# Two sums of weights from DRAM for one unit of a feed-forward layer, and other starting points for all such sums

## The chip, the cores and the metric

The kernel runs on one core of one Trainium2 chip. The metric is the device time of one execution in microseconds, as the median of several runs. The core has TensorE (PE in the profile; its weight loads are PEld), VectorE (DVE), ScalarE (ACT), GpSimd (POOL) and the queue of SyncE (SP), which issues most of the DMAs. The DMAs of all queues run on the core's 16 DMA engines.

## The reference

The reference computes two layers of an encoder over 256 positions of width 2048, in float32. Layer 0 mixes positions by pooling and attention, layer 1 by a bidirectional mLSTM; each is followed by the same kind of gated feed-forward block:

```
def conv_ffn(x, w_up, conv_w, conv_b, w_down):
    u = x @ w_up
    up = jnp.pad(u, ((0, 0), (1, 1), (0, 0)))
    c = conv_w.astype(u.dtype)
    u = c[0] * up[:, :-2] + c[1] * up[:, 1:-1] + c[2] * up[:, 2:] + conv_b.astype(u.dtype)
    gate, val = jnp.split(u, 2, axis=-1)
    return (jax.nn.silu(gate) * val) @ w_down
```

`w_up` is 2048 x 11264, `w_down` 5632 x 2048. The change concerns the product `x @ w_up` of both layers, and in layer 0 how one fifth of a part of it gets its weights.

## The kernel before

**Weights.** All weights are float32 and are streamed once, in 890 chunks of 128 x 1024 (512 KB), by the class `Stream`. `load` issues the DMA of a chunk from SP (L93 where the chunk is put together from parts, L99 else). `split` turns it into a high part (a rounding cast on ScalarE, L152) and a low part (a subtraction on VectorE, L153); both are multiplied, so that each product is three matmuls (high x high, high x low, low x high). Loads run 5 to 7 chunks ahead of TensorE, splits 2 to 3.

**Order.** TensorE's instructions stand in the order in which the code writes them. VectorE, ScalarE, SP and POOL are ordered by a scheduler that estimates times, except where the code says `keep_in_program_order`.

**Layers in terms of loads.** Loads 0 to 79 are the attention layer's, 80 to 403 the first feed-forward layer's, 404 to 565 the mLSTM layer's, 566 to 889 the second feed-forward layer's.

**Units.** Most of the up-projection goes column block by column block (`up`, tile `up`). Five groups of four column blocks per layer, the units, go in another way (`quads`, tile `p`): the product of 2 x 2 blocks is made with seven block products instead of eight, from sums of blocks of the activations (tile `sx`) and sums of blocks of the weights. For each of eight pairs of rows a unit has the four weight blocks b11, b12, b22, b21 side by side in the input `in_q` (128 x 2048), and needs

- an even chunk: b11 and s1 = b11 + b12,
- an odd chunk: s2 = b22 + s1 and s3 = b21 + s2,
- a left chunk: b12 + b22 beside b22 (one addition on VectorE, L140), and every two pairs a last chunk without sums.

**Where the sums are made.** `UNITS` lists the five units of each layer; the last number of an entry, in the code `made` or `kind`, says where. With 2, all three sums s1, s2, s3 are made in DRAM ahead of time: SP copies blocks of the input into a buffer G in DRAM (L121, L123), and POOL issues DMAs that add to it (L124 for s1 in two halves of 64 partitions, L128 for s2 and for s3). The even chunk is then loaded as b11 from the input and s1 from G, the odd chunk whole from G. With 3, as the third unit of layer 0 has it, only s1 is made in DRAM, and the odd chunk is loaded raw (b22, b21) and gets its sums by two additions on VectorE, one after the other (L142, L143):

```
if kind == "chain":
    pin(add(l, l, self.sum))
    pin(add(r, r, l))
```

**When the sums are made.** `places` gives for each pair a load and a gap; the pair's four steps (first half, second half, s2, s3) are issued right behind the loads number at, at + gap, at + 2 gap and at + 3 gap, by `make_step`. SP only copies; each accumulate on POOL waits for the copies, or for the accumulate before it, and everything behind it on POOL waits too. In the attention and mLSTM layers POOL also does the small power operations of the norms (L275). A load that reads G waits on SP for its accumulate.

## Time and profile before

| | |
|---|---|
| median of 3 runs | 2162.97 us (2162.5 to 2164.91) |
| the profiled execution | 2164.07 us, span 2162.3 us |
| TensorE busy | 2155.0 us |
| VectorE, ScalarE, POOL busy | 1716.1, 1308.5, 276.0 us |
| bytes by DMA | 596.15 MB |
| of those by POOL's queue | 59.00 MB |
| mean granted TensorE clock | 0.999 |

The page of the profile has the engines' busy times, the DMA queues and the costliest groups of instructions. A row of a group names line, engine, operation and tile, the shapes and the count, then busy time and mean duration, then the idle time of the engine before these instructions and what ended it. A row of the timeline begins with the start and the length in microseconds. A row of the windows gives a stretch, its length, for each engine busy time and count, and at the end the granted clock, the mean busy share of the 16 DMA engines and the GB/s that they moved. An arrow `<-` names what a thing was made from, or what an engine waited for.

### The profile page before, as it was taken

The numbers are of one execution on the slowest core, as the hardware profiler recorded it, in microseconds if no ns is written. First come the engines' busy times: TensorE is split into PE (matmuls) and PEld (weight loads), VectorE is DVE, ScalarE is ACT, GpSimd is POOL, SyncE is SP. The second block draws the span as 40 slices with busy tenths as digits, with TensorE's granted clock in tenths as the row PEclk, the third lists the DMA queues.
The fourth block names the chain that finished last, engine by engine and source line by source line (L and its number), as shares of the span: only waits on it lengthen the run. The fifth ranks groups of instructions, "written<-read, shape, count | busy, mean of one in ns | idle before, by whom it ended". The sixth has DMA issues, their size and how long they took to land.

```text
span 2162.3 us, 31058 instructions
## 1 busy us (share of the span) xinstructions
PE 2155.0 (100%) x10896; PEld 1827.3 (85%) x10896; DVE 1716.1 (79%) x2400; ACT 1308.5 (61%) x1840; POOL 276.0 (13%) x344
## 2 busy tenths in 40 slices
PE   9999999999999999999999999999999999999999
PEld 7888888888888888889888888888888888888887
DVE  7686698989888797866777676669898888879785
ACT  7665566766556576656554544456676666757663
POOL 0222111211111111101111111110000000000000
PEclk9999999999999999999999999999999999999999
DMA  9878899999999999979899988877999999877773
GB/s 327 256 226 247 253 262 329 336 329 315 311 328 297 360 312 348 315 207 249 250 268 247 259 249 247 259 243 223 312 284 309 301 294 291 272 253 235 260 244 119
DMA packets 204702, 596.15 MB, mean 276 GB/s; under 512 B 26010, under 2 KB 28354, under 8 KB 204546
## 3 DMA queue, kind: packets, MB, share of 16 engines
q1 hardware_dynamic: 167776, 531.43, 70.1%
q0 software_dynamic: 33696, 59.00, 18.6%
q10 hardware_dynamic: 3074, 3.75, 0.9%
q8 instruction: 85, 1.39, 0.2%
q14 instruction: 71, 0.58, 0.1%
HBM read 591.93 MB, written 119.58 MB: 329 GB/s over the span
## 4 chain that ended last, share of the span: by engine, by line
PE 99%; DVE 1%; issue 0%; ACT 0%; DVEq 0%; ACTq 0%
PE up L268 25%; PE dn L268 21%; PE p L268 17%; PE op L268 8%; PE mv L268 4%; PE mk L268 4%; PE mq L268 4%; PE mo L268 4%; PE qproj L268 3%; PE kproj L268 1%; PE pool L268 1%; PE vproj L268 1%; PE tr L1081 1%; PE av L268 1%; PE qk L268 1%; PE end L268 1%
## 5 line engine op out<-in xcount | busy, mean ns | idle before, releaser
L153 DVE TENSOR_TENSOR hl<-w,hl 128x1024 fp32r<-128x1024 f32 (+2 forms) x892 | 1074.0, 1217 | 323.0 <-ACT hl L152 309.0
L152 ACT CAST hl<-w 128x1024 fp32r<-128x1024 f32 (+2 forms) x891 | 923.5, 1048 | 641.3 <-PE dn L268 105.0
L268 PE MATMUL up<-xx,hl 128*128 128x512 f32 (+1 forms) x3072 | 560.7, 337 | 0.0
L268 PEld LDWEIGHTS up<-xx,hl 128*128 128x128 f32 x3072 | 486.8, 188 | 76.7
L268 PE MATMUL dn<-hl,g 128*128 128x512 f32 x2064 | 492.0, 391 | 0.0
L268 PEld LDWEIGHTS dn<-hl,g 128*128 128x128 f32 x2064 | 386.1, 188 | 79.4
L268 PE MATMUL p<-hl,sx 128*128 128x512 f32 x960 | 250.4, 390 | 1.9 <-DVE hl L153 1.9
L124 POOL DMA_DIRECT2D G<-in_q x160 | 132.1, 827 | 881.0 <-DMA G<-in_q 877.4
L268 PEld LDWEIGHTS p<-hl,sx 128*128 128x128 f32 x960 | 175.9, 188 | 36.6 <-DVE hl L153 2.9
L128 POOL DMA_DIRECT2D G<-G x144 | 127.3, 884 | 530.7 <-DMA G<-in_q 228.2
L268 PE MATMUL p<-hl,xx 128*128 128x512 f32 x720 | 193.7, 391 | 0.0
L268 PEld LDWEIGHTS p<-hl,xx 128*128 128x128 f32 x720 | 131.1, 188 | 24.2
L268 PE MATMUL mk<-xx,hl 128*128 128x512 f32 (+1 forms) x512 | 92.5, 338 | 0.0
L268 PE MATMUL mq<-xx,hl 128*128 128x512 f32 (+1 forms) x512 | 92.2, 337 | 0.0
L268 PE MATMUL mv<-hl,xx 128*128 128x512 f32 (+2 forms) x480 | 91.7, 350 | 0.0
L268 PE MATMUL op<-hl,cat 128*128 128x512 f32 x384 | 91.6, 393 | 0.0
L268 PE MATMUL mo<-hl,xx 128*128 128x512 f32 x384 | 90.5, 391 | 0.0
L268 PE MATMUL op<-hl,mcat 128*128 128x512 f32 x384 | 89.5, 392 | 0.0
L268 PEld LDWEIGHTS mq<-xx,hl 128*128 128x128 f32 x512 | 79.3, 188 | 11.6
L268 PEld LDWEIGHTS mk<-xx,hl 128*128 128x128 f32 x512 | 79.0, 188 | 11.7 <-DVE hl L153 0.4
L268 PEld LDWEIGHTS mv<-hl,xx 128*128 128x128 f32 x480 | 78.3, 189 | 11.2
L268 PEld LDWEIGHTS op<-hl,mcat 128*128 128x128 f32 x384 | 71.5, 188 | 14.6
(242 smaller groups left out, 1861.5 us busy)
## 6 DMA issues: line engine op xcount, KB each, us to landing
w<-in_up SPq DMA_DIRECT2D x192, 512.0 KB, 6.2
w<-in_dn SPq DMA_DIRECT2D x176, 512.0 KB, 6.1
w<-in_m_in SPq DMA_DIRECT2D x124, 512.0 KB, 5.9
w<-in_q SPq DMA_DIRECT2D x88, 512.0 KB, 6.3
G<-in_q SPq DMA_DIRECT2D x144, 256.0 KB, 6.5
G<-G POOLq DMA_DIRECT2D x144, 256.0 KB, 7.5
w<-G SPq DMA_DIRECT2D x72, 512.0 KB, 6.5
w<-in_a_in SPq DMA_DIRECT2D x46, 512.0 KB, 6.1
```

The source lines that it names most:

```text
L124: pin(add.dma_start(G[r, 0:512], src[r, 512:1024], accum_op=ALU.add))
L128: pin(add.dma_start(G[:, at : at + 512], G[:, of : of + 512], accum_op=ALU.add))
L152: (self.nc.vector.tensor_copy if i + c == 0 else self.nc.scalar.copy)(hl[:, 0, c : c + n], w[:, c : c + n])
L153: self.nc.vector.tensor_sub(hl[:, 1, c : c + n], w[:, c : c + n], hl[:, 0, c : c + n].bitcast(F32))
L268: pe.matmul(out_, lhsT, rhs, start=start, stop=stop, skip_group_check=True)
L1081: pe.transpose(tr[:, j, t * P : t * P + P], src[:, c : c + P], ident)
```

## The change

A fourth value of `made` is introduced and given to the third unit of layer 0. With 4, s1 and s2 are made in DRAM. The copy of the first two steps also takes b22 (a further 128 KB each), step three adds s1 to it, step four does nothing. The odd chunk is loaded in two parts of 256 KB, s2 from G and b21 from the input, and VectorE makes s3 with one addition. The even chunk stays as it was.

The places of all pairs of layer 0 and of the first 28 pairs of layer 1 are changed as well. In layer 0 the first pair begins behind load 16 in place of 24, and the steps of the first unit follow every 5.5 loads in place of 6.5, of the second every 8 in place of 9, of the third every 6 in place of 4 with a gap of 3 in place of 2, of the fourth every 10 as before and 8 loads sooner, of the fifth every 9 in place of 8. Of layer 1's pairs, 4 in place of 7 begin in the first feed-forward layer, and 24 in place of 21 in the mLSTM layer; the last 12 stay.

```diff
-        if kind in ("made", "have"):
+        if kind in ("made", "have", "half"):
...
                 pin(sync.dma_start(G[r, 0:512], src[r, 0:512]))
-                if kind == 2:
-                    pin(sync.dma_start(G[r, 1024:2048], src[r, 1024:2048]))
+                if kind in (2, 4):
+                    to = 2048 if kind == 2 else 1536
+                    pin(sync.dma_start(G[r, 1024:to], src[r, 1024:to]))
                 pin(add.dma_start(G[r, 0:512], src[r, 512:1024], accum_op=ALU.add))
-        elif kind < 3:
+        elif kind < 3 or kind == 4 and part == 2:
...
+            if kind == "half":
+                pin(add(r, r, l))
...
-    ((1, 1, 17, 38, 2), (2, 1, 45, 64, 2), (3, 1, 71, 97, 3), (4, 1, 104, 127, 2), (5, 1, 134, 157, 2)),
+    ((1, 1, 17, 38, 2), (2, 1, 45, 64, 2), (3, 1, 71, 97, 4), (4, 1, 104, 127, 2), (5, 1, 134, 157, 2)),
...
-                seq.append(("made", ((key, 2, 4),)) if made in (1, 2) else ("chain", q[:, 1024:2048]))
+                seq.append(("half", ((key, 2, 3), q[:, 1536:2048])) if made == 4 else
+                           ("made", ((key, 2, 4),)) if made in (1, 2) else ("chain", q[:, 1024:2048]))
...
-    places = [[(24 + 13 * k // 2, 3) for k in range(8)] + [(76 + 9 * k, 4) for k in range(8)]
-              + [(150 + 4 * k, 2) for k in range(8)] + [(180 + 10 * k, 5) for k in range(8)]
-              + [(264 + 8 * k, 4) for k in range(8)]]
+    places = [[(16 + 11 * k // 2, 3) for k in range(8)] + [(60 + 8 * k, 4) for k in range(8)]
+              + [(122 + 6 * k, 3) for k in range(8)] + [(172 + 10 * k, 5) for k in range(8)]
+              + [(256 + 9 * k, 4) for k in range(8)]]
     at = len(weights) + len(ml)
-    places.append([(at - 240 + 11 * k, 5) for k in range(7)] + [(at - 162 + 38 * k // 5, 4) for k in range(21)]
+    places.append([(at - 220 + 14 * k, 5) for k in range(4)] + [(at - 164 + 20 * k // 3, 4) for k in range(24)]
                   + [(at + 17 * k, 8) for k in range(12)])
```

## The prediction

> **What bounds the kernel now.** First the page, for the engines and the DMA queues.

> ```profile
> PE 2155.0 (100%) x10896; PEld 1827.3 (85%) x10896; DVE 1716.1 (79%) x2400; ACT 1308.5 (61%) x1840; POOL 276.0 (13%) x344
> q1 hardware_dynamic: 167776, 531.43, 70.1%
> q0 software_dynamic: 33696, 59.00, 18.6%
> ```

> TensorE is busy for 2155.0 of 2162.3 us. A change elsewhere pays only where TensorE waits or its clock falls, and costs only where it makes TensorE wait. Second, the waits of TensorE and of its weight loads (us in total, times, longest).

> ```profile
> PE p L268 <- DVE hl L153: 1.9, 1, 1.9
> PEld mk L268 <- DVE hl L153: 0.4, 1, 0.4
> ```

> Behind the start there is one true stall: a product of a four-column unit (tile p) waits 1.9 us for VectorE's low half of a split chunk. Third, the two feed-forward layers over like stretches, from a like piece of up-projection to a like piece: columns are length, busy us and instructions of PE, PEld, DVE, ACT, POOL, then clock, DMA share and GB/s.

> ```profile
> 357.36:906.84 549.48, 547.59 (x2702) 461.79 (x2701) 474.29 (x617) 351.20 (x452) 90.36 (x112) 1.00 1.02 327
> 1550.76:2096.22 545.46, 545.46 (x2701) 460.82 (x2701) 464.92 (x600) 350.87 (x450) 30.09 (x37) 1.00 0.87 277
> 568.00:572.00 4.00, 2.11 (x9) 1.43 (x8) 4.00 (x6) 0.97 (x4) 1.61 (x2) 0.94 1.05 353
> 572.00:576.00 4.00, 4.00 (x13) 3.11 (x13) 2.40 (x3) 1.86 (x2) 0.00 (x0) 0.63 1.01 253
> ```

> The same TensorE work (2702 and 2701 matmuls) takes 549.48 us in the first layer and 545.46 in the second: 4.02 us more. They lie in the last two rows: 1.89 us of idleness between 568 and 572, and behind it a lowered clock, 4 us at 0.94 and 4 at 0.63, which is 4 x 0.06 + 4 x 0.37 = 1.72 us of lost matmul time. That is 3.61; the rest of the 4.02 is smaller hiccups. The first layer's DMA engines are full (share 1.02), the second's are not (0.87). Fourth, VectorE's order before the stall.

> ```profile
> 562.76 0.68 DVE L142 TENSOR_TENSOR w<-w,w 128x512 f32<-128x512 f32 x1
> 564.16 1.22 DVE L153 TENSOR_TENSOR hl<-w,hl 128x1024 fp32r<-128x1024 f32 x1
> 565.29 0.68 DVE L143 TENSOR_TENSOR w<-w 128x512 f32<-128x512 f32 x1
> 566.69 2.35 DVE L153 TENSOR_TENSOR hl<-w,hl 128x1024 fp32r<-128x1024 f32 x2
> 568.96 0.68 DVE L142 TENSOR_TENSOR w<-w,w 128x512 f32<-128x512 f32 x1
> 569.56 1.22 DVE L153 TENSOR_TENSOR hl<-w,hl 128x1024 fp32r<-128x1024 f32 x1
> 570.83 0.30 PEld L268 LDWEIGHTS p<-hl,sx 128*128 128x128 f32 x2 [2.31 <-DVE hl L153]
> ```

> L142 and L143 are the two chained additions of an odd chunk of the third unit. They are 2.53 us apart, another chunk is split between them, and the split that TensorE waits for ends at 569.56 + 1.22 = 570.78.

> **The change, part by part.**

> (1) One addition less per odd chunk. The group rows for the chain are these.

> ```profile
> L142 DVE TENSOR_TENSOR w<-w,w 128x512 f32<-128x512 f32 x8 | 5.5, 683 | 0.0
> L143 DVE TENSOR_TENSOR w<-w 128x512 f32<-128x512 f32 x8 | 5.5, 684 | 0.1
> ```

> VectorE loses 8 x 0.683 = 5.5 us of work. On the late path lie two of the eight, at 562.76 and 568.96, worth 1.37 us: alone they leave 1.89 - 1.37 = 0.5 us of the stall. But the chunk is also whole after one addition, at about 563.4 rather than at 565.29 + 0.68 = 565.97, so its split can go 2.5 us sooner, in its own turn. 1.37 + 2.5 is over 1.89, so I take the stall as gone. The end on the other side: 0.5 us of idleness stays and lowers the clock again for 1.7, leaving a gain of 4.0 - 2.2 = 1.8. With both ends, 1.8 to 4.0; I take 4.0. What is late next is the following odd chunk:

> ```profile
> 572.87 2.36 DVE L153 TENSOR_TENSOR hl<-w,hl 128x1024 fp32r<-128x1024 f32 x2 [0.82 <-ACT hl L152]
> 580.45 0.53 PEld L268 LDWEIGHTS p<-hl,sx 128*128 128x128 f32 x3
> ```

> Its split ends at 572.87 + 1.2 = 574.1, with two additions in front of it; TensorE takes it at 580.45, or 4.0 sooner without the stall, at 576.4. That still fits.

> Does the clock belong to the stall? The row 572 to 576 says so: 0.63 directly behind 1.89 us of idleness, 1.00 elsewhere in the stretch. [...]

> (2) The odd chunk becomes two transfers, one half from the input, one from G. Rows of both sizes:

> ```profile
> w<-in_q SPq DMA_DIRECT2D x88, 512.0 KB, 6.3
> w<-in_q SPq DMA_DIRECT2D x80, 256.0 KB, 5.9
> w<-G SPq DMA_DIRECT2D x80, 256.0 KB, 6.3
> ```

> Two halves land no later than a whole (5.9 and 6.3 against 6.3). SP issues 8 more; the G half waits for its POOL sum, whose last step now stands 65 to 81 loads ahead of it. Cost nothing, hidden by the loads ahead; if that cover were gone, everything behind it on SP would wait.

> (3) A second sum in DRAM: per pair one copy (two halves of 128 KB more from SP) and one 256 KB accumulate on POOL. The price of DMA time follows from q1 and q0: 0.701 x 2162.3 / 531.43 = 2.85 us of all sixteen engines per MB copied, 0.186 x 2162.3 / 59.00 = 6.82 per MB accumulated. A pair adds 0.262 MB of each: 2.53 us, eight pairs 20.3 us. The issues fall into two queues, SP's (first row: what it waits for, total, times, longest) and POOL's (count | busy, mean ns | idle before):

> ```profile
> SPq L99 <- DVE hl L153: 1048.7, 569, 6.9
> L128 POOL DMA_DIRECT2D G<-G x144 | 127.3, 884 | 530.7 <-DMA G<-in_q 228.2
> ```

> SP waits 1048.7 us for free buffers, so 16 more small copies, and copies moved to other places, cover none of its useful time. POOL mostly stands waiting for its own copies; in the feed-forward layer only further sums are queued behind it, so eight more cost TensorE nothing by themselves.

> (4) Sums begun at other times. A full pair (three blocks of 0.262 MB copied and three accumulated) costs 7.6 us, a new pair of the third unit 5.1, an old one 2.5. Per load that is: second unit 0.84 before (one in 9 loads), 0.95 after (one in 8); third unit 0.63 before (one in 4), 0.85 after (one in 6). Loads 100 to 176 are used by TensorE from about 311 to 470 us (matmuls counted along its instructions). Loads 100 to 122 gain 22 x 0.11 = 2.4 us, 150 to 176 gain 26 x 0.22 = 5.7, and at the change-over last steps of the second unit fall beside first ones of the third, by my count 1 us: some 9 in all. Three pairs, 23 us, move from the end of the first feed-forward layer into the mLSTM layer. Where the load is heaviest:

> ```profile
> 324.00:378.00 54.00, 54.00 (x270) 45.70 (x269) 44.40 (x54) 34.41 (x43) 8.87 (x11) 1.00 1.04 330
> 690.00:770.00 80.00, 80.00 (x384) 67.22 (x384) 64.69 (x77) 47.64 (x57) 13.87 (x17) 1.00 1.05 347
> w<-in_up SPq DMA_DIRECT2D x16, 512.0 KB, 9.3
> w<-in_up SPq DMA_DIRECT2D x12, 512.0 KB, 10.1
> 351.18 1.22 DVE L153 TENSOR_TENSOR hl<-w,hl 128x1024 fp32r<-128x1024 f32 x1
> 354.25 1.77 PEld L268 LDWEIGHTS dn<-hl,g 128*128 128x128 f32 x8
> PEld p L268 <- DVE hl L153: 0.4, 1, 0.4
> ```

> Rows three and four are the landing times within 320 to 400 and within 690 to 770; then one chunk of the tight place, split by 352.40 and first used at 354.25, so 2 us ready; last, the only wait of a weight load in 340 to 400. The engines are full in 324 to 378 and TensorE is not idle. In 690 to 770 the fifth unit's sums are already begun every 8 loads, at a share of 1.05 and landings of 10.1 us, and TensorE is busy in all 80 us. So 9 us more, spread over 160, is most likely paid from the loads' lead. Bounds: 0 to 9 us of lateness, less the 2 us by which chunks lie ready there. I take 0, nearest to the 690 to 770 row, which has this density.

> (5) Attention. The first copies go out behind load 16, the second of the four in the first row below, at about 28 us, and not behind load 24; their accumulate on POOL then stands ahead of the small power operations there.

> ```profile
> 26.66 9.62 SPq L99 DMA_DIRECT2D w<-in_a_in  x4
> x<-in_xn SPq DMA_DIRECT2D x4, 512.0 KB, 9.5
> 28.00:46.00 18.00, 18.00 (x81) 14.93 (x80) 12.52 (x24) 15.14 (x39) 1.76 (x3) 1.00 0.93 357
> 45.90 2.45 POOL L275 TENSOR_TENSOR ry_qk<-rv_qk,mhalf 128x8 f32<-128x8 f32 x1
> 50.39 1.29 DVE L516 TENSOR_TENSOR rot_k<-rot_k,re_qk 128x512 f32<-128x512 f32 x2
> 52.47 0.60 PE L525 MATMUL tr_k<-cst,rot_k 128*128 128x128 f32 x4
> ```

> The keys' scale ends on VectorE at 51.68, TensorE takes it at 52.47: 0.8 us of room. A copy that lands in some 10 us, as the blocks of x do just before it, is there by 38, and its accumulate is out of POOL's way. The second half goes with load 19, near 38, and lands by 48 at the latest. If its accumulate is put ahead of ry_qk, that is up to 48 + 0.9 - 45.9 = 3 us late, and TensorE 2.2; if behind, nothing. I take 0: in the code the operation comes before load 19.

> (6) mLSTM. One spot has no room:

> ```profile
> 1015.12 1.15 DVE L829 SCALAR_TENSOR_TENSOR arg<-G,mc,kml 128x256 f32<-128x256 f32 x3 [1.21 <-DMA G<-gd]
> 1016.79 1.22 DVE L153 TENSOR_TENSOR hl<-w,hl 128x1024 fp32r<-128x1024 f32 x1
> ```

> VectorE waits for the gates' broadcast, and the split behind it is the one that a weight load awaits for 0.4 us. A later broadcast passes straight to TensorE; an earlier one gains at most those 0.4. The sums there are denser by one in seven: 0.4 gained to 2 lost; I take 0, as the copies also fall on other loads.

> Sum: -4.0. Against the profiled execution, 2164.07 - 4.0 = 2160.07. That execution lies 1.10 above the median of the runs; if the 4.0 come off the median whole, 2158.97. I take the middle, **2159.5 us**, 0.16% faster, inside the 0.2% (4.3 us) that a measurement can tell from no change. Even the whole 4.02 is 0.19%.

> **Rivals.**

> The loads become late (slower). Place: first and second unit of the first layer, loads 100 to 176. With the engines full, the 9 us pass on; 2 us are eaten by the chunks that lie ready; 7 reach TensorE in two stalls, each with a lowered clock of 1.7: 10.4 lost, 4.0 gained, 2162.97 + 6.4 = 2169.4; I take 2168.5, as some of it is made up where the share falls. For it: share 1.04 and the weight load that already waits 0.4 us. Against it: the 690 to 770 row. It decides once 4.9 us reach TensorE (4.9 + 3.4 - 4.0 = 4.3). Chance 0.24.

> The stall shrinks or moves: the third unit's one addition is again placed late in VectorE's order, or another chunk takes its place. 0.5 us idle plus the clock: 2162.97 - 1.8 = 2161.2, and no gain, 2163, if a full stall comes back. Chance 0.16.

> Only the idleness counts. If the lowered clock was particular to the profiled run, the gain is 1.9: 2161.1. For it: the runs shown spread from 2162.5 to 2164.91. [...] Against it: the clock row. Chance 0.10.

> A small new stall in attention or mLSTM (parts 5 and 6), 1 to 2 us with or without the clock: 2159.5 + 2 = 2161.5. Chance 0.10.

> **How the numbers follow.** My forecast has 0.40, by itself 2158.0 to 2161.0. Faster by over 0.2% means below 2158.6: only the low end of my own case, 0.11. Slower means above 2167.3: the late loads and a little of two others, 0.26. Within: 0.63. The range runs from 2158.2 (4.0 off the median and 0.8 of the runs' spread) to 2169.0, just past the late-load case; about 0.06 below and 0.13 above are left out.

> **What would show it.** Right: no wait of PE p on DVE hl around 570, clock 1.00 there, a stretch from 357 to 907 of about 545.5 us; one addition of 0.68 per odd chunk, VectorE 5.5 us less busy; accumulates G<-G 152 instead of 144, 2.1 MB more in each of q0 and q1; waits for loads in 320 to 400 longer, TensorE not idle. Wrong: a new PE wait between 340 and 480 with a lowered clock behind it; PE idle at tr_k near 52 or at mk near 1018; the p wait still there with the split of the odd chunk out of turn.

## The result, and the profile after

The changed kernel takes 2169.05 us (median of 17 runs, 2165.02 to 2173.56), the kernel before 2164.04 on the same chip (17 runs, 2162.5 to 2167.82). The ratio is 1.0023 with a 95% interval of 1.0016 to 1.0031: 5 us slower. Forecast were 2159.5, and 2169.0 as the range's upper end. The runs of the changed kernel also lie further apart, over 8.5 us against 5.3.

The page of the changed kernel first (engines with share of the span and instructions; the two main DMA queues with packets, MB and share).

```profile
PE 2155.3 (99%) x10896; PEld 1827.1 (84%) x10896; DVE 1710.9 (79%) x2392; ACT 1308.0 (60%) x1840; POOL 282.7 (13%) x352
q1 hardware_dynamic: 170208, 533.52, 70.3%
q0 software_dynamic: 34848, 61.10, 19.0%
```

What the change does to the work is as forecast: VectorE 5.2 us less, eight accumulates more on POOL, 2.1 MB more in each queue. TensorE is busy as long as before, in a span that is 4.4 us longer (2166.7). The waits of TensorE, by line and releaser (us in total, times, longest):

```profile
PE p L271 <- DVE hl L156: 2.5, 3, 1.1
PE up L271 <- DVE xx L337: 1.7, 2, 1.2
PE npr L271 <- DVE dg L363: 0.5, 1, 0.5
PE ov L271 <- DVE pt L572: 0.5, 1, 0.5
PE ov L271 <- ACT pt L571: 0.5, 1, 0.5
```

In place of one stall of 1.9 us there are these smaller ones, and a further row of 0.2 us (p <- ACT hl). Tile ov is a product of the attention, up one of the up-projection, p one of a unit; npr carries the layer norm's scale. Both kernels also wait 1.2 us at their start (wps). The like stretches of the two feed-forward layers (columns as in the prediction), and the place of the old stall, which now lies 4.4 us later:

```profile
361.72:911.32 549.60, 546.85 (x2701) 460.57 (x2701) 469.37 (x610) 351.32 (x452) 80.80 (x100) 1.00 1.00 321
1555.37:2100.87 545.50, 545.50 (x2702) 460.81 (x2701) 464.90 (x600) 350.90 (x450) 30.07 (x37) 1.00 0.86 277
572.00:576.00 4.00, 4.00 (x20) 3.30 (x19) 4.00 (x7) 2.64 (x4) 0.79 (x1) 1.00 1.07 351
576.00:580.00 4.00, 4.00 (x20) 3.30 (x18) 2.54 (x4) 1.98 (x3) 0.00 (x0) 1.00 0.99 314
```

The old stall is gone, and its lowered clock: TensorE is busy at 1.00 in all 8 us. Yet the first layer's stretch is no shorter, 549.60 against 549.48: 2.75 us of new idleness stand in it. And it begins 361.72 - 357.36 = 4.36 us later. So all of the profiled 4.4 us are lost ahead of this stretch, and within it the gain from the old stall is given back. Matched chunk by chunk (the first matmul of a load's chunk in both traces), TensorE comes 1.3 us later than in the kernel before to load 82, 4.4 later to loads 90 to 130, 8.3 later to loads 145 to 220, and 4.5 later from load 230 on. Where, the order of time shows: first TensorE ahead of the stretch, then POOL and VectorE, then the weight loads in the stretch.

```profile
158.79 0.39 PE L271 MATMUL ov<-pt,vt 128*128 128x256 f32 x1 [0.51 <-ACT pt L571]
159.70 0.50 PE L271 MATMUL ov<-pt,vt 128*128 128x256 f32 x2 [0.53 <-DVE pt L572]
...
268.29 0.96 PE L271 MATMUL up<-xx,hl 128*128 128x512 f32 x4 [1.24 <-DVE xx L337]
269.80 0.67 PE L271 MATMUL npr<-dg,cst 128*128 128x256 f32 x2 [0.54 <-DVE dg L363]
...
272.36 0.85 PE L271 MATMUL up<-xx,hl 128*128 128x512 f32 x3 [0.51 <-DVE xx L337]
```

```profile
264.90 0.79 POOL L125 DMA_DIRECT2D G<-in_q  x1 [8.87 <-DMA G<-in_q]
265.43 1.00 POOL L278 TENSOR_TENSOR ry_n<-rv_n,mhalf 128x2 f32<-128x2 f32 x1
266.47 0.16 DVE L280 TENSOR_TENSOR re_n<-ry_n 128x2 f32<-128x2 f32 x1 [5.45 <-POOL ry_n L278]
```

```profile
382.79 0.99 PEld L271 LDWEIGHTS p<-hl,sx 128*128 128x128 f32 x5 [1.39 <-DVE hl L156]
...
393.95 0.99 PEld L271 LDWEIGHTS p<-hl,sx 128*128 128x128 f32 x5 [1.26 <-DVE hl L156]
...
404.39 1.00 PEld L271 LDWEIGHTS p<-hl,sx 128*128 128x128 f32 x5 [0.90 <-DVE hl L156]
```

Three places, then: 158 (about 1 us more than before), the layer norm at 266 to 272 (about 3 us, 2.3 of them as plain idleness in these rows), and the second unit of the first feed-forward layer at 381 to 404 (about 4 us). At the layer norm POOL has stood 8.87 us on an accumulate that waits for its copy; behind it stands ry_n, the power operation of the layer norm's scale, whose input VectorE had written by 261.0, and which runs at 265.43. VectorE, which needs its result next, stands 5.45 us, and TensorE then waits for VectorE's xx. In the kernel before the operation runs in front of the accumulate that comes next:

```profile
260.05 0.72 POOL L275 TENSOR_TENSOR ry_n<-rv_n,mhalf 128x2 f32<-128x2 f32 x1 [3.83 <-DVE rv_n L273]
265.26 0.86 POOL L124 DMA_DIRECT2D G<-in_q  x1 [4.50 <-DMA G<-in_q]
```

Scale of the comparisons below: three kernels that were taken twice came back within 0.1, 0.4 and 1.3 us, and the 95% intervals against the kernel before reach some 2 us to either side. A difference of less than 2 us between two of the kernels is therefore not shown by itself, and pieces of the change do not add up more closely than that.

### The profile page after: what moved, and what is told of

It is laid out like the page before. It is cut to its first block, busy times and chain, and to the rows that moved or that the text cites. A ratio compares the mean times of both kernels' runs of the same rounds, so it can differ in the third digit from the quotient of the medians.

```text
span 2166.7 us, 31105 instructions
## 1 busy us (share of the span) xinstructions
PE 2155.3 (99%) x10896; PEld 1827.1 (84%) x10896; DVE 1710.9 (79%) x2392; ACT 1308.0 (60%) x1840; POOL 282.7 (13%) x352
## 4 chain that ended last, share of the span: by engine, by line
PE 91%; DMA 6%; DVE 2%; ACT 1%; issue 0%; POOL 0%; ACTq 0%; SPq 0%; DVEq 0%; POOLq 0%
PE up L271 23%; PE dn L271 21%; PE p L271 16%; PE op L271 7%; PE mo L271 4%; PE mk L271 4%; PE mq L271 4%; PE mv L271 4%; PE qproj L271 3%; DMA w<-in_up 1%; PE kproj L271 1%; DMA w<-in_q 1%; PE vproj L271 1%; DMA G<-in_q 1%; DMA w<-G 1%; PE tr L1084 1%
## 5 line engine op out<-in xcount | busy, mean ns | idle before, releaser
L129 POOL DMA_DIRECT2D G<-G x152 | 142.4, 937 | 429.8 <-DMA G<-in_q 213.5
## 6 DMA issues: line engine op xcount, KB each, us to landing
w<-in_up SPq DMA_DIRECT2D x192, 512.0 KB, 6.1
w<-in_dn SPq DMA_DIRECT2D x176, 512.0 KB, 5.6
w<-in_m_in SPq DMA_DIRECT2D x124, 512.0 KB, 6.5
w<-in_q SPq DMA_DIRECT2D x80, 512.0 KB, 6.0
G<-G POOLq DMA_DIRECT2D x152, 256.0 KB, 7.7
G<-in_q SPq DMA_DIRECT2D x144, 256.0 KB, 6.1
w<-G SPq DMA_DIRECT2D x72, 512.0 KB, 6.2
w<-in_a_in SPq DMA_DIRECT2D x46, 512.0 KB, 7.5
```

The source lines that it names most:

```text
L129: pin(add.dma_start(G[:, at : at + 512], G[:, of : of + 512], accum_op=ALU.add))
```

## Experiments

| Kernel | what differs | median, us (runs) | ratio to before, 95% |
|---|---|---|---|
| changed kernel | | 2169.05 (17) | 1.0016 to 1.0031 |
| e1_half_alone | second sum, old times | 2172.38 (5) | 1.0033 to 1.0058 |
| e2_times_alone | new times, one sum | 2167.58 (11) | 1.0012 to 1.0030 |
| e5_one_addition | before, less eight additions | 2160.58 (11) | 0.9978 to 0.9996 |
| e3_pool_order | changed, one pair a load later | 2166.79 (11) | 1.0004 to 1.0022 |
| e4_scale_load | changed, two attention pairs later | 2167.66 (11) | 1.0008 to 1.0025 |
| e6_again | changed kernel again | 2168.61 (11) | 1.0011 to 1.0029 |
| e7_third_spread | second sum, spread over later loads | 2160.94 (11) | 0.9982 to 1.0000 |
| e12_spread_again | the same again | 2162.28 (11) | 0.9987 to 1.0004 |
| e8_third_later | second sum from load 136 | 2167.06 (11) | 1.0003 to 1.0021 |
| e10_no_last_add | e3 less eight accumulates | 2164.36 (11) | 0.9997 to 1.0014 |
| e11_early_spread | new times for two units, spread | 2164.12 (11) | 0.9993 to 1.0011 |
| e9_spread_layer2 | e7 with the second layer's new times | 2163.67 (12) | 0.9997 to 1.0013 |
| e14_layer2_alone | before, second layer's new times | 2165.87 (11) | 1.0001 to 1.0019 |
| e15_layer2_old | changed, second layer's old times | 2166.59 (11) | 1.0007 to 1.0024 |
| e17_layer1_alone | before, first layer's new times | 2165.08 (11) | 0.9999 to 1.0017 |
| e13_two_pairs | second sum for two pairs, old times | 2161.54 (11) | 0.9982 to 1.0000 |
| e16_one_pair | second sum for one pair, old times | 2160.35 (11) | 0.9977 to 0.9994 |
| e18_one_pair_again | the same again | 2160.45 (11) | 0.9983 to 1.0000 |

The kernel before had medians of 2163.25 to 2163.79 beside the experiments.

**The two halves of the change.** e1_half_alone has the second sum and the old times, e2_times_alone the new times and one sum.

```diff
# e1_half_alone, against the changed kernel (second layer's list likewise)
-    places = [[(16 + 11 * k // 2, 3) for k in range(8)] + [(60 + 8 * k, 4) for k in range(8)]
-              + [(122 + 6 * k, 3) for k in range(8)] + [(172 + 10 * k, 5) for k in range(8)]
+    places = [[(24 + 13 * k // 2, 3) for k in range(8)] + [(76 + 9 * k, 4) for k in range(8)]
+              + [(150 + 4 * k, 2) for k in range(8)] + [(180 + 10 * k, 5) for k in range(8)]
# e2_times_alone, against the changed kernel: the old unit, and the code for it
-    ((1, 1, 17, 38, 2), (2, 1, 45, 64, 2), (3, 1, 71, 97, 4), ...
+    ((1, 1, 17, 38, 2), (2, 1, 45, 64, 2), (3, 1, 71, 97, 3), ...
```

> The changed kernel with all sums in DRAM begun at the old times; only the third unit of the first layer keeps its second sum. Theory 'places' (the loss comes from the new times, at three places: 1.3 us at 158, 3.1 us at 267 to 272, 3.9 us at 381 to 404): none of the three stalls, and the old stall at 570 with its lowered clock is gone too, so about 3.9 us below the kernel before, 2160, and VectorE 5.5 us less busy. Rival 'second sum' (the 20 us of added DMA time make the loads late): stalls of a p tile or others between 380 and 600 remain and the time is 2164 or more. Rival 'the stall only moves': one stall of 0.5 to 2 us near 570, 2161 to 2164.

> The kernel before with the new times in both layers; the third unit keeps its one sum. Theory 'places': all three new stalls (8.3 us together) and the old one at 570 with its clock (3.9 us): 2164 + 8.3 = 2172, the stall at 570 smaller only if the lateness ahead of it gives VectorE room. Rival 'second sum': the new times cost little, 2164 to 2166, no stall at 381 to 404.

Measured 2172.38 and 2167.58: both theories miss on the first. The second sum at the old times is the worst kernel of all. The two longest of TensorE's waits (first fence), and those of ScalarE's casts for loads between 430 and 520 us (second fence):

```profile
PE p L271 <- DVE hl L156: 3.2, 3, 1.9
PE up L271 <- ACT hl L155: 2.7, 1, 2.7
```

```profile
ACT hl L155 <- DMA w<-G: 15.9, 8, 5.9
ACT hl L155 <- DMA w<-in_up: 9.9, 6, 4.1
ACT hl L155 <- DMA w<-in_dn: 4.4, 4, 2.1
```

ScalarE waits 30 us for loads in that stretch; the kernel before has no such wait there. A pair every 4 loads at 5.1 us is more than the loads can bear. In e2_times_alone the stall at 570 and the one at the layer norm are there, but none at 377 to 404. So the four kernels make a square: 2164 with neither part, 2172.4 and 2167.6 with one, 2169.05 with both. The new times make the second sum bearable without making it free (the last step, 1.5 us, is within the noise, but a gain of 3 from the stall should have come there).

**One addition less, and nothing else.** The first addition of the chain is left out in e5_one_addition.

```diff
             if kind == "chain":
-                pin(add(l, l, self.sum))
                 pin(add(r, r, l))
```

> The kernel before with the first of the two chained additions of each odd chunk of the first layer's third unit left out (a part of the sum is then missing from those chunks); no transfer is added or moved. Theory 'addition' (step 1 of the prediction: one addition less removes the whole stall at 570 and its lowered clock, and the loss of the change comes from transfers alone): no wait of a p tile at 570, clock 1.00 there, 2163.8 - 3.9 = 2160. Rival 'the split stays late in VectorE's order': a wait of 0.5 us and more stays at 570, 2161.5 to 2163.5.

Measured 2160.58, 3.2 us under the kernel before. No p tile waits at 570. Step 1 stands: VectorE's chain was the stall, and one addition less clears it.

**POOL's order, and the attention's transfer.** Each moves pairs of the changed kernel by one load.

```diff
# e3_pool_order
-[(60 + 8 * k, 4) for k in range(8)]
+[(60 + 8 * k + (k == 3), 4) for k in range(8)]
# e4_scale_load
-[(16 + 11 * k // 2, 3) for k in range(8)]
+[(16 + 11 * k // 2 + (k > 5), 3) for k in range(8)]
```

> The changed kernel with one pair of the second unit (its fourth) begun one load later, so that the power operation of the layer norm stands ahead of that pair's accumulate in POOL's order. Theory 'places': the stalls at 266.8 to 272 go and 3.1 us with them, less what the loads in 381 to 404 lose of the time that the stalls gave them: 2166 to 2167.5 in place of 2169. Rival 'loads alone' (only the DMA time counts; TensorE makes up at 381 to 404 what it lost at 267): the stalls at 267 go, those at 381 to 404 grow by as much, 2169.

> The changed kernel with the last two pairs of the first unit begun one load later, so that no copy is issued between the transfer of inv and its landing. Theory 'places': inv lands in about 5.1 us and not 6.4, VectorE does not wait the extra 1.3 us, TensorE does not stall at 158, and the time falls by 1.3 us to 2167.7 or less. Rival (the landing of inv is not set by that copy): inv lands in 6.4 us again, TensorE stalls 1.3 us at 158, 2169.

e3_pool_order: 2166.79. POOL's rows around the layer norm and the whole list of TensorE's waits:

```profile
260.32 0.72 POOL L278 TENSOR_TENSOR ry_n<-rv_n,mhalf 128x2 f32<-128x2 f32 x1 [4.05 <-DVE rv_n L276]
266.18 0.86 POOL L125 DMA_DIRECT2D G<-in_q  x1 [5.15 <-DMA G<-in_q]
```

```profile
PE p L271 <- DVE hl L156: 3.0, 3, 1.8
PE wps L295 <- DVE pad L664: 1.2, 1, 1.2
PE mk L271 <- DVE hl L156: 0.8, 1, 0.8
PE ov L271 <- DVE pt L572: 0.5, 1, 0.5
```

The power operation runs 5 us sooner, the waits of up and npr are gone, and the time is 2.3 us under the changed kernel's first figure and 1.8 under its second (e6_again, below). One load more or less at one pair decides it. e4_scale_load is inconclusive: inv, an input of the pooling that is loaded there, landed in 5.5 us, and TensorE stalled 0.3 us at 158. But with the new times unaltered inv landed in anything from 5.1 to 6.3 us (eight profiles, TensorE idle by 0 to 0.9 us), and with the old ones from 4.8 to 6.0 (six). The stall at 158 is mostly a spread of landings between executions and not the change.

**The changed kernel once more.**

> The changed kernel once more, unaltered, for a second profile. Theory 'jitter' (landings differ from execution to execution; the stalls at 158 and at 381 to 404 are where little room is left, and come in some executions only; the one at 267 is an order and comes in each): the stalls at 266 to 272 come again with 2.5 to 4 us, those at 381 to 404 and 158 have other sizes or stand at other chunks, median near 2169. Rival 'fixed': all stalls again within 0.3 us of the first profile.

Measured 2168.61. The stalls at 266 to 272 and at 381, 392 and 403 all came again, within about 0.5 us: "fixed" is nearer than "jitter". But in e4_scale_load, with the same second sum, there was none at 381 to 404, and a wait of 3.1 us at mk instead: at a lead of 5 to 7 us there (below) a chunk was late in four of five profiles with that sum at the new times, and in this one not.

**How much of a second sum the loads can bear.** Four kernels move or cut the added DMA time.

```diff
# e7_third_spread and e12_spread_again: e1_half_alone with
-(150 + 4 * k, 2) ... (180 + 10 * k, 5)
+(150 + 6 * k, 3) ... (196 + 8 * k, 4)
# e8_third_later: e3_pool_order with
-(122 + 6 * k, 3) ... (172 + 10 * k, 5)
+(136 + 6 * k, 3) ... (180 + 10 * k, 5)
# e10_no_last_add: e3_pool_order with
-        elif kind < 3 or kind == 4 and part == 2:
+        elif kind < 3:
# e11_early_spread: e3_pool_order with the third and fourth unit of e7_third_spread, the rest old
```

> The third unit's second sum kept, the first, second and fifth units and the second layer begun at the old times; the third unit's pairs begun every 6 loads from 150 on (in place of every 4) and the fourth unit's every 8 from 196 on. DMA time of sums per load is then 0.85 in 150 to 196 and 0.95 in 196 to 260. Theory 'density' (the stalls of the second sum come where sums take over about 1 us of DMA time per load, and the new times cost TensorE at the layer norm): no stalls at 444 to 500, none at 267, 2160 to 2162, faster than the kernel before. Rival 'amount' (the 20 us of added DMA time must be paid wherever they stand while the engines are full): stalls of 3 us and more between 440 and 600, 2166 and more.

> e7_third_spread once more, unaltered, for a closer figure and a second profile: 2160 to 2162, 0.1 to 0.2% under the kernel before; no stall over 1 us behind the start. Against it: 2163 and more, which would make the gain seen before a chance.

> The changed kernel with the second unit's fourth pair begun one load later (POOL's order mended at the layer norm), the third unit's pairs begun every 6 loads from 136 on in place of 122, and the fourth unit's from 180 on as before. Theory 'density': no stall at 267; the loads 120 to 140 get 10 us of DMA time back, the stalls at 381 to 404 go; 2161 to 2163. Rival 'amount': the lateness only moves to later chunks, stalls of 2 to 4 us between 400 and 520, 2165 to 2167.

> As e3_pool_order, with the last accumulate of each second sum of the third unit left out (eight accumulates of 256 KB, 14 us of DMA time at 6.8 us per MB; a part of the sum is then missing from those chunks); the copies stay. Theory 'lead' (the second sum's DMA time eats the lead of the loads 120 to 150): the lead there rises from 6 to 7 us and more, the stalls at 377 to 404 and 511 go, 2161 to 2163. Rival (the copies, or the order on VectorE, make the stalls): 2166 to 2167 as e3_pool_order.

> The new times for the first two units with POOL's order mended, the spread times of e7_third_spread for the third and fourth, the old times for the fifth and for the second layer. Theory 'lead': the first two units' sums are out of the way before load 130, the third's begin at 150 only, so chunks 130 to 150 have a lead of 10 us and more and no later ones under 7; 2160 to 2161, no stall between 200 and 900. Rival 'order' (the new times of the first units hurt by themselves): stalls of 1 us and more in 310 to 410, 2163 and more.

All 20 us of DMA time are borne nearly without loss when they lie behind load 150: 2160.94 and 2162.28, under the kernel before, and 0.4 and 1.7 us over e5_one_addition; their profiles have one stall, of 0.6 and 0.9 us, near 509. The rival "amount" falls. But "density" falls too: e8_third_later has the same one pair in 6 loads and loses (2167.06). By the forecast's prices its densest ten loads between 130 and 200 take 1.01 us of DMA time each for sums, as those of e7_third_spread do. What tells the kernels apart is the lead of the loads, the time from a chunk's landing to its first use by TensorE, as medians over the chunks named (worked out from the loads whose landing the traces have):

| chunks | before | e2 | changed | e6 | e8 | e1 | e7 |
|---|---|---|---|---|---|---|---|
| 120 to 129 | 6.0 | 6.8 | 6.4 | 6.5 | 7.2 | 9.0 | 8.9 |
| 130 to 139 | 6.0 | 8.4 | 5.5 | 6.4 | 12.7 | 9.7 | 9.5 |
| 140 to 149 | 6.7 | 10.3 | 6.7 | 6.2 | 11.0 | 9.8 | 9.5 |
| 160 to 169 | 13.5 | 14.3 | 9.1 | 11.1 | 10.8 | 4.1 | 12.6 |
| 170 to 179 | 9.6 | 11.5 | 8.4 | 10.2 | 5.6 | 3.4 | 8.0 |
| 180 to 189 | 10.9 | 13.6 | 12.1 | 13.5 | 5.6 | 6.2 | 9.2 |

Where the median is near 6 us or lower, TensorE stalls in the changed kernel at 381 to 404, in e8 at 480 to 515 and in e1 at 444 to 500. The kernel before has 6 us at chunks 120 to 149 and just gets by. That is one profile: nine others with the same transfers up to load 150 have 7.3 to 10.0 there, so such a median is good to some 2 us. At chunks 130 to 149 the two profiles of the new times with one sum (e2_times_alone, e17_layer1_alone) have 8 to 10.5, no less than the old times give. The five with the second sum besides (changed kernel, e6_again, e3_pool_order, e4_scale_load, e15_layer2_old) have 5 to 7. So it is the second sum at these places that takes the lead.

The median does not tell everything. e4_scale_load has 6.6 and no stall there. Near 510 a stall of 0.6 to 1.6 us comes at medians of 6.5 to 9.3, where ScalarE waits for one load (3.8 us for one of in_b in e3_pool_order). And why e8_third_later has less lead than e7_third_spread stays open.

In the page's own terms the lead is seen in ScalarE's waits for loads between 320 and 410 us, here of the changed kernel, of e2_times_alone and of e7_third_spread:

```profile
ACT hl L155 <- DMA w<-in_up: 8.1, 6, 2.6
ACT hl L155 <- DMA w<-in_dn: 6.7, 4, 2.3
ACT hl L155 <- DMA w<-G: 5.0, 5, 2.6
ACT hl L155 <- DMA w<-in_b: 2.0, 1, 2.0
```

```profile
ACT hl L152 <- DMA w<-G: 4.7, 5, 1.4
ACT hl L152 <- DMA w<-in_dn: 3.2, 2, 2.1
ACT hl L152 <- DMA w<-in_up: 0.9, 2, 0.7
```

```profile
ACT hl L155 <- DMA w<-G: 1.3, 1, 1.3
ACT hl L155 <- DMA w<-in_b: 0.9, 1, 0.9
```

21.8 us, 8.8 and 2.2. The kernel before has 14.0, the nine others with its transfers there 0.6 to 8.5. Of the five with the second sum at the new times four have 17.6 to 21.8, and e4_scale_load, the one without a stall, has 6.0.

e10_no_last_add gains 2.4 us on e3_pool_order, between the two theories: the stall at 511 went, those at 355 to 388 shrank to 2 us in all, and the lead of chunks 140 to 149 rose from 6.7 to 9.2. e11_early_spread is 1.8 us slower than e12_spread_again beside it, though its profile has no stall in 310 to 500; it has waits of 0.6 us at 510, of 1.1 at 772 and of 0.8 each at mk and in the attention, which neither theory named.

**The second layer's times.** e9_spread_layer2 has them over e7_third_spread, e14_layer2_alone over the kernel before; e15_layer2_old is the changed kernel without them.

```diff
-    places.append([(at - 240 + 11 * k, 5) for k in range(7)] + [(at - 162 + 38 * k // 5, 4) for k in range(21)]
+    places.append([(at - 220 + 14 * k, 5) for k in range(4)] + [(at - 164 + 20 * k // 3, 4) for k in range(24)]
```

> As e7_third_spread, with the second layer's sums begun at the new times (4 pairs in the last part of the first feed-forward layer in place of 7, the rest in the mLSTM layer). Theory (step 6 of the prediction: the mLSTM takes the three moved pairs at no cost): 2161, within 1 us of e7_third_spread run beside it, the split behind the gates' broadcast at about 1018 late by 0 to 1 us as in the kernels with the old times. Rival 'broadcast': the denser sums delay the gates' broadcast, TensorE waits 1 to 3 us at mk with a lowered clock in some executions, 2162.5 to 2165.

> The kernel before with the new times in the second layer alone. Theory (step 6 of the prediction): no change, 2163.3 to 2164.3. Rival 'broadcast' (denser sums in the mLSTM delay the gates' broadcast for mk at 1018 more often): 2164.5 to 2166, TensorE waits 1 us and more at mk in the profile.

> The changed kernel with the old times in the second layer. Theory (the loss is the first layer's): 2168 to 2169.5, stalls at 267 to 272 and at 377 to 404 as before. Rival 'broadcast': 1.5 us and more under the changed kernel, 2166.5 to 2167.5.

Alone they cost 2.5 us (2165.87 against 2163.39, interval 0.2 to 4.1); over e12_spread_again, measured beside it, 1.4; and without them the changed kernel is 2.0 to 2.5 us under its two figures. None of the three is far clear of the noise, but all point the same way. The profile of e14_layer2_alone shows the spot of step 6 (mk is a product for the mLSTM's keys):

```profile
1017.18 1.15 DVE L829 SCALAR_TENSOR_TENSOR arg<-G,mc,kml 128x256 f32<-128x256 f32 x3 [3.81 <-DMA G<-gd]
1018.24 0.69 DVE L433 TENSOR_TENSOR tb_q<-mq,tb_q 128x512 f32<-128x512 f32 x1
...
1018.84 1.22 DVE L153 TENSOR_TENSOR hl<-w,hl 128x1024 fp32r<-128x1024 f32 x1
...
1020.11 1.00 PEld L268 LDWEIGHTS mk<-xx,hl 128*128 128x128 f32 x6 [2.09 <-DVE hl L153]
```

The gates' broadcast lets VectorE go at 1017.18, 2.06 us later than in the kernel before (1015.12), the split follows at 1018.84 and the weight load waits 2.09 us in place of 0.4. That the denser sums make it late is likely but not shown: e13_two_pairs, with the old times, has the same wait with 2.5 us in its profile, while the changed kernel's own shows 0.5. Over all 20 profiles the weight load at mk waits 1.5 us on average with the new times (nine, 0 to 3.5) and 0.8 with the old (eleven, 0 to 2.5). So the spot holds some 0.7 us of the cost; where the rest of it lies is not seen.

**The first layer's times without POOL's order and without the second sum.**

```diff
# e17_layer1_alone, against the kernel before: the changed kernel's first-layer list, with
+[(60 + 8 * k + (k == 3), 4) for k in range(8)]
```

> The kernel before with the new times in the first layer alone, POOL's order at the layer norm mended (the second unit's fourth pair one load later), and one sum in the third unit. Theory (of the first layer's new times only POOL's order and the second sum's DMA time cost): within 1 us of the kernel before, 2162.8 to 2164.5, no stall at 267 nor at 377 to 404, the stall at 570 there with 1.9 us. Rival (the times cost by themselves): 2165 and more.

Measured 2165.08: at the lower edge of the rival. Its profile shows no stall at 267 nor at 377 to 404, so neither mechanism is at work. Of the 1.8 us over the kernel before, some 0.7 are the lowered clock behind the stall at 570, which by their mean clock of 0.999 9 of its 11 executions have and 4 in 10 of the kernel before, at 1.7 us each; the rest has no place, and the interval just reaches 1.

**The second sum where the stall is.** The stall at 570 belongs to one odd chunk, of the fifth pair. e13_two_pairs sums twice in DRAM for the fifth and sixth pair, e16_one_pair for the fifth alone; all times are old.

```diff
# e16_one_pair, against e1_half_alone (e13_two_pairs: HALF = ("031_4", "031_5"))
-    ((1, 1, 17, 38, 2), (2, 1, 45, 64, 2), (3, 1, 71, 97, 4), ...
+    ((1, 1, 17, 38, 2), (2, 1, 45, 64, 2), (3, 1, 71, 97, 3), ...
+HALF = ("031_4",)
...
             q, key = four[u, at], f"{layer}{c}{i}_{at}"
+            made = 4 if key in HALF else made
```

> The kernel before, all times old, with the second sum in DRAM for two pairs of the third unit alone (the fifth and sixth, whose odd chunks the stall at 570 belongs to): 2 x 2.53 = 5.1 us of DMA time added in place of 20.3. Theory 'lead' (the gain is one chunk's addition, the loss the DMA time that all eight sums take from the loads): no stall at 570, none at 444 to 500, 2160 to 2161.5. Rival (any added sum at this place makes the loads late, as e1_half_alone): stalls of 1 us and more in 440 to 520, 2163.5 and more.

> As e13_two_pairs with the second sum for the fifth pair alone, 2.5 us of DMA time. Theory 'lead': the stall at 570 belongs to this chunk, so 2160 to 2161 as with the addition left out, unless the next odd chunk, which still has two additions, becomes the late one (then a stall of up to 1 us near 576, 2162 to 2163). Rival: the stall needs all additions gone, 2163.5.

> e16_one_pair once more, unaltered, for a closer figure of the kernel that beats both: 2160 to 2161.5, 0.1 to 0.15% under the kernel before. Against it: 2162.5 and more, which would make the first figure a chance.

Measured 2161.54, 2160.35 and 2160.45. The profile of e13_two_pairs, of its slowest execution (2165.41), has stalls of 0.2 us at 483 and 1.6 at 510, as its rival had it, and 2.1 at mk, though its median goes with the theory; the one-pair kernels have none in 440 to 520. One pair gives the gain of all eight, as much as e5_one_addition, for 2.5 us of DMA time in place of 20.3. All of TensorE's waits in e16_one_pair, the first of them at the start, and the stretch of the first feed-forward layer:

```profile
PE wps L295 <- DVE pad L664: 1.2, 1, 1.2
PE mk L271 <- DVE hl L156: 0.2, 1, 0.2
```

```profile
357.36:906.84 549.48, 549.48 (x2724) 464.25 (x2723) 475.76 (x622) 352.69 (x455) 92.03 (x114) 1.00 1.02 329
```

TensorE does not idle in the layer: in the same 549.48 us it gets 2724 matmuls done, where the kernel before did 2702. This kernel beats both, at 0.9985 (0.9977 to 0.9994) and, taken again, 0.9991 (0.9983 to 1.0000) of the kernel before.

## Why the prediction was wrong, step by step

(1) One addition less: right in kind, a third too large. The stall goes whole, as e5_one_addition shows without any transfer and e16_one_pair with one pair's. The gain is 2.8 to 3.2 us, not 4.0, since the lowered clock comes only in some executions: of 149 executions of the kernel before beside the experiments, 59 have a mean clock of 0.999 and a median of 2164.47, 90 have 1.000 and 2162.80. Of the 22 of e5_one_addition and e16_one_pair, where the stall is gone, none has 0.999, and one of the 11 of e18_one_pair_again has. The forecast charged its 1.7 us whole; the rival "only idleness counts" left it out whole; it is worth about 0.7.

(2) Two loads for a chunk: no run tried it alone. e16_one_pair and e5_one_addition are within 0.3 us of each other, so for one chunk it costs nothing that shows.

(3) The second sum, "eight more cost TensorE nothing by themselves", with its 20.3 us of DMA time left to step (4): this step failed. The DMA time was priced about right (the page of the changed kernel gives 2.85 and 6.74 us per MB against 2.85 and 6.82), but not what it buys from. At the old times eight second sums cost the 8.6 us of e1_half_alone and the lost gain besides. At the new times they cost the difference between a gain of 3 that should have come on top of e2_times_alone and a loss of 1.5 that did: 4.5 us, good to some 2. In the two profiles of the changed kernel 3.9 and 3.8 us are lost at 381 to 404.

(4) The new times in the first layer, "most likely paid from the loads' lead", priced at nothing after the stretch 690 to 770: failed together with (3). That stretch was the wrong yardstick. It has the same DMA share (1.05 against 1.04) and landings no earlier (median 9.8 us from the issue against 9.5), but its chunks land some 8 us ahead of their use; those of 347 to 401 us land 6 ahead, and at 5 to 7 stalls were seen. The forecast's 2 us of ready chunks there were seen and then set aside. It also had the place of the added time wrong. By its own prices and the two lists of places, the change adds 10 us of DMA time between loads 100 and 150 and under 1 between 150 and 176, where the forecast counted 3.4 and 5.7. So nearly all of it falls on the chunks with the least lead. The rival "loads become late" named the place, but that its 2168.5 lies near the result is luck: it summed 7 us and two lowered clocks there, less a gain of 4.0, and the profile has 3.9 us there without a lowered clock; half of the loss is elsewhere. With one sum the new times add nothing in loads 100 to 150 (39 us against 40) and cause no stall there (e2_times_alone), so the mechanism is theirs and the second sum's together.

(5) Attention: the right mechanism at the wrong operation. The forecast examined POOL's ry_qk at 46 us, which did not come late, and did not look at ry_n, a later power operation on the same queue, at 260 us. It belongs to the norm in front of the first feed-forward layer, while the forecast had only further sums queued on POOL in that layer, and the text ahead of it named power operations in the attention and mLSTM layers alone. There an accumulate moved in front: 3 us in the profile, about 2 in the medians (e3_pool_order). The rows at 264.90 and 265.43 show it: an 8.87 us wait for a copy holds back an operation that needs no copy.

(6) mLSTM: the spot, the chain and the range (-0.4 to +2) were right, the value taken, 0, was not. The new times of the second layer cost 1.4 to 2.5 us in three comparisons, some 0.7 of it seen at the spot. Taking the middle of a range whose far side is +2, where no room is left, would have been nearer.

The sum then: about -3 from (1), +4.5 from (3) and (4), +2 from (5), +2 from (6), 5.5 in all; 5.0 were measured. Each piece is good to 1 or 2 us only, so that the agreement is closer than it has a right to be. The pieces do not add up exactly: e17_layer1_alone would put up to 1.8 more on top, while e2_times_alone, which has (5), (6) and that, lies only 3.8 over the kernel before. What stays open is that last piece, and how far the broadcast's lateness is the denser sums' doing.

## What to carry to other kernels

Before you call added DMA time hidden, take the lead of the loads at the tightest chunks (landing to first use) and not the share of the DMA engines. Here stalls came at a lead of about 6 us, while the share was 1.03 to 1.05 with stalls and without. Take it from more than one profile, since the same transfers gave medians from 6 to 10 us. When DMA issues that wait for data share an engine's queue with small compute operations, follow every such operation along the whole queue, because a move by one load can put a wait of several us in front of it (8.87 us at the layer norm here). And cure a single late chunk at that chunk: one pair in eight held the whole gain.

## What the hardware showed that was not expected

```profile
568.16:571.58 3.42, 1.75 (x7) 0.90 (x5) 3.19 (x4) 1.90 (x3) 0.79 (x1) 1.00 1.02 372
571.58:574.99 3.41, 3.14 (x14) 2.61 (x15) 2.58 (x5) 2.40 (x3) 0.00 (x0) 1.00 1.04 347
```

```profile
265.25:268.67 3.42, 1.74 (x9) 1.22 (x8) 3.40 (x12) 1.73 (x3) 0.89 (x1) 1.00 0.58 159
268.67:272.08 3.41, 3.41 (x11) 2.86 (x11) 3.41 (x4) 1.08 (x2) 0.79 (x1) 0.50 0.91 206
```

```profile
265.92:269.33 3.41, 2.10 (x11) 1.47 (x9) 2.85 (x9) 1.06 (x3) 0.97 (x2) 1.00 0.50 101
269.33:272.74 3.41, 2.43 (x12) 2.00 (x13) 3.41 (x6) 1.76 (x2) 1.07 (x2) 1.00 0.96 252
```

```profile
1018.85:1022.26 3.41, 0.86 (x5) 0.78 (x6) 3.41 (x7) 2.17 (x3) 1.63 (x2) 1.00 0.33 117
1022.26:1025.68 3.42, 3.42 (x13) 2.93 (x12) 3.42 (x4) 2.54 (x4) 0.00 (x0) 0.50 0.65 176
```

In these profiles the edge lies between 1.67 and 1.68 us of idleness, about half a window, and the price is one window at half clock, 3.41 x 0.5 = 1.7 us of work. So the same stall lowers the clock or not, by whether it falls into one window or across two: the kernel before has all 1.89 us of the stall at 570 in one window (568.14 to 571.55) and 0.50 in the next, e17_layer1_alone has it with 1.9 us, 1.67 of them in one window, and no lowered clock. It also means that stalls of about 1 us that fall into one window cost more than their idleness, as those of 1.15 and 0.54 us in the first window of e2_times_alone do, and that stalls spread over more windows, as in the changed kernel, where the four with the most idleness have 0.98 to 1.31 us each, cost no clock at all (1.00 behind each).
